# Pauses of the merged streams per head and per pair, and small products of a hybrid decoder step in column groups

## The chip, the cores and the metric

One core of a Trainium2 chip runs the whole step. The metric is the device time of one execution in microseconds (us). Its engines are named as in the profile: PE (TensorE, matmuls), PEld (its weight loads), DVE (VectorE), ACT (ScalarE), POOL (GpSimd), SP (the queue that issues most DMAs).

## The reference, cut to what matters

One layer of a decoder, for a prompt (16 meta tokens and 512 tokens) and for 8 samples of 8 new tokens each with 2048 cached tokens in pages. Both share all weights. Tokens in all: 512 + 64 + 16 = 592.

```
xn = rmsnorm(x) ; h = xn @ w_in                        # one projection, D = 1024 -> 5640
q, k, v | gdn_qkv, gdn_z, gdn_b, gdn_a | gate_a, gate_b = split(h)
# branch a: differential attention, 4 heads, two maps of 64
a   = softmax(q1 k1') - lam * softmax(q2 k2') ; o_a = rmsnorm(a @ v)
# branch b: gated DeltaNet, 4 heads of 128
qkv = silu(causal_dwconv(gdn_qkv, width 4))            # its last 3 rows are an output
gq, gk = l2norm(.) ; beta = sigmoid(gdn_b)
g   = -exp(a_log) * softplus(gdn_a + dt_bias)          # log decay per token and head
gcum = cumsum(g)  ; decay = exp(gcum_i - gcum_j)       # within a chunk
solve (I + lower(beta k k' * decay)) [u, w] = [beta v, beta k exp(gcum)]
v_new = u - w @ S ; o = (q exp(gcum)) @ S + (q k' * decay) @ v_new
S = S exp(g_last) + (k exp(g_last - gcum))' @ v_new
o_b = rmsnorm(o) * silu(gdn_z)
# merge and FFN
mix = sigmoid(gate_a) * (o_a @ w_a) + sigmoid(gate_b) * (o_b @ w_b)
x  += rmsnorm(mix @ w_out)
x  += rmsnorm((gelu(causal_dwconv(gate)) * up) @ w_down)
```

Each sample brings its own state S (128x128 per head) and each prompt head starts from zero. Everything is fp32 to the outside.

## The kernel before

Activations lie with channels on partitions and tokens along the free dimension. Big products are made in fp32r (one pass) on numbers split into a high part `hi` and a rest `lo`: `hi*hi + hi*lo + lo*hi`, three matmuls for one (`project`, `dense_steps`). A product whose operands are plain fp32 is shown by the profile as two matmul rows.

The program is written as Python generators that are merged into one order. Each `yield d` in a stream says: `d` us of PE work of other streams shall be placed before this stream goes on. `merge` counts PE work as it is emitted (`self.work`: 0.00042 us per moving column for fp32r and for products of at most 32 stationary columns, 0.00168 for other fp32 ones, 0.11 per transpose) and takes, of the streams whose pause is over, the one with the least work done against its weight. The pauses come from one table, `DELAY`, by number. Within this order the framework places the instructions on each engine, and every engine then runs in order.

Stages in order:

- `embed`: load x, normalise, transpose, first query products.
- `da_queries`, `gdn_scalars` (beta and g for all heads: `w_in`'s eight columns for b and a against all tokens, in two halves of 256 and 336), `gdn_consts`.
- Two merged streams. `main` (weight `MAIN_1`, later `MAIN_2`): keys, values and prompt attention of four heads, then the four GDN heads one after another (`gdn_chain`), each merged with the projection of the next head (`gdn_project`). `rest` (weight `REST_W`): attention of the samples in four pairs over the paged cache (`sample_attention`), the gates, and branch a.
- `mix`, `out_proj`, `ffn_in`, `ffn_out`.

In `gdn_chain` for one head: row sums of the decays by a product of `ones` with `gu` (the upper triangle times g), exponentials on ACT, transposes of k, q, v, norms by `rsqrt` (an add on DVE and a power on POOL), `kn` (normalised k) and its transpose `kk`, the triangular solve, then the states of the samples: `zk` holds k and q of the eight samples in a block layout, and eight products of `zk` with the eight states accumulate in one PSUM tile. After that four chunks of the prompt follow one another. Behind them stand the gate (`gdn_gate`) and the transposes of the output `on` into `ob`.

`conv_tile` runs the width-4 convolution of one 128-channel tile (three per head: k, q, v) and keeps the last rows in `tail`; its inner function `rest` transposes `tail` and writes it out on POOL's DMA queue.

Of the kernel before, what the change touches and what calls it, by code (L numbers as in the profile page):

```python
# [9 lines left out]
F32 = mybir.dt.float32  # L10
# [41 lines left out]
def _lay_out_constants():  # L52
# [14 lines left out]
    put("ones", np.ones((128, 128)))  # L67
# [27 lines left out]
    put("zero", np.zeros((128, 1)))  # L95
    put("causal", np.where(i[None, :] > i[:, None], NEG, 0.0))
# [35 lines left out]
    13.61, 3.59, 0.94, 0.6, 6.0, 1.52, 1.66, 1.43, 1.32, 1.05, 0.93, 0.17, 26.0, 0.69, 0.9, 0.77,  # L132
    0.09, 0.85, 0.38, 2.28, 0.14, 0.6, 0.74, 2.36, 6.91, 0.77, 1.4, 5.18, 1.38, 1.46, 12.26,
# [15 lines left out]
REST_W = 165.0  # L149


class Body:
# [39 lines left out]
    def run(self):  # L192
# [6 lines left out]
        self.ident = self.consts[:, 0:128]  # L199
        self.mhalf = self.t(self.cpool, [128, 32], "mhalf")  # L200
# [313 lines left out]
    def gdn_scalars(self, pool):  # L514
# [74 lines left out]
        )  # L589

    def gdn_decays(self):
# [46 lines left out]
    def conv_tile(self, ps, ch, dp, dt):  # L638
# [12 lines left out]
        tail = self.t(pool, [128, 27], "tail", bufs=2)  # L651
        nc.scalar.copy(tail[:, 0:3], pb[:, CS - 3 - o : CS - o])
        nc.scalar.copy(
            tail[:, 3:27].rearrange("p (b j) -> p b j", b=NB),
            pb[:, CS - o : CM - o].rearrange("p (b t) -> p b t", b=NB)[:, :, TS - 3 :],
        )

        def rest():
            tp = self.ps("t")
            self.transpose(tp[:27, :128], tail)  # L660
            rows = self.t(pool, [27, 128], "tailT", bufs=2)
            nc.vector.tensor_copy(rows, tp[:27, :128])
            sl = slice(128 * ch, 128 * ch + 128)
            nc.gpsimd.dma_start(self.o["new_gdn_conv_prompt"][0, 0, :, sl], rows[0:3])
            nc.gpsimd.dma_start(self.o["new_gdn_conv_sample"][0, :, :, sl].rearrange("b j c -> (b j) c"), rows[3:27])

# [19 lines left out]
        return rest  # L686
# [12 lines left out]
    def gdn_project(self, h, st):  # L699
# [8 lines left out]
        rest = None  # L708
        for part in (1, 0, 2):
# [24 lines left out]
    def gdn_chain(self, h, st):  # L734
# [4 lines left out]
        def cols(ap, h=h):  # L739
# [26 lines left out]
        self.mm(rp, self.c("ones"), gu, start=True, stop=True)  # L766
# [27 lines left out]
        yield DELAY[2]  # L794
# [7 lines left out]
        yield DELAY[3]  # L802
# [5 lines left out]
        for e in range(2):  # L808
            self.rsqrt(rr[:, e], ss[:, e], 0.25, EPS, 128, 5)
# [8 lines left out]
        yield DELAY[4]  # L818
# [1465 lines left out]
```

## Time and profile before

| | |
|---|---|
| time, median of 3 runs | 1135.83 us (1135.69 to 1139.21) |
| profiled execution, its own time | 1136.37 us |
| its span | 1134.6 us |
| PE busy, 8263 matmul rows | 1112.5 us |
| PEld busy | 976.8 us |
| DVE busy | 729.3 us |
| ACT busy | 524.7 us |
| POOL busy | 225.8 us |
| HBM over the span | 137 GB/s |

How to read the profile: the span goes from the first to the last instruction of the program. A group of instructions shows line, engine, operation, `out<-in` by the program's names, shapes (for PE: contraction*stationary columns, then the moving operand), count, busy time, mean time of one, idle time of the engine before it and what ended it. In an answer in order of time the first two numbers are start and length. A PE row is longer than its share of PE, because matmuls overlap; the distance from start to start tells the cost. `L273` is the one line that issues every product, `L421` the one that issues every transpose, so PE's groups are told apart by tiles.

### The profile page before, as it was taken

The page shows a single profiled execution, that of the slowest core. Times are in us where ns is not written, and L with a number is a line of the kernel's source. Part 1 is how long each engine was busy: PE and PEld are TensorE (multiplying, and loading weights), DVE is VectorE, ACT ScalarE, POOL GpSimd, SP SyncE. Part 2 cuts the span into 40 slices and gives each one's busy share as a digit, 9 for nine tenths or more (in the row PEclk, how much of TensorE's full clock was granted, in tenths as well). Part 3 has the DMA queues.
Part 4 walks back from the last instruction along what each step waited for, and adds up shares of the span by engine and source line. Part 5 has one row for each costly group of instructions (what it writes and reads, how often), then busy time and mean ns, then how long its engine had stood idle before and what let it go on. Part 6 is the DMA issues. An engine that isn't in the chain of part 4 may idle for free.

```text
span 1134.6 us, 22730 instructions
## 1 busy us (share of the span) xinstructions
PE 1112.5 (98%) x8263; PEld 976.8 (86%) x8263; DVE 729.3 (64%) x1891; ACT 524.7 (46%) x1264; POOL 225.8 (20%) x344
## 2 busy tenths in 40 slices
PE   8999999999999999999999999999999999999997
PEld 6987887787787787689999987899999999988886
DVE  5456666696486377375335575599999999752315
ACT  5244544464365365352324244464555555842311
POOL 3122221020120020010000003344444454300000
PEclk9999999999999999999999999999999999999999
DMA  6376336837846866733234344333333332333213
GB/s 193 83 235 199 102 92 200 261 103 251 246 147 224 283 178 223 251 87 87 50 90 118 105 146 135 102 102 95 94 95 95 95 100 84 116 108 108 84 48 120
DMA packets 167610, 156.97 MB, mean 138 GB/s; under 512 B 12540, under 2 KB 123715, under 8 KB 167498
## 3 DMA queue, kind: packets, MB, share of 16 engines
q1 hardware_dynamic: 162833, 147.14, 42.5%
q0 software_dynamic: 3264, 5.16, 1.5%
q10 hardware_dynamic: 1400, 3.22, 0.9%
q8 instruction: 65, 1.06, 0.4%
q14 instruction: 48, 0.39, 0.1%
HBM read 145.60 MB, written 9.88 MB: 137 GB/s over the span
## 4 chain that ended last, share of the span: by engine, by line
PE 82%; DVE 7%; issue 3%; ACT 3%; POOL 3%; DMA 2%; SPq 0%; DVEq 0%; POOLq 0%; ACTq 0%
PE ps_d L273 32%; PE ps_t L273 20%; PE ps_g L273 16%; PE ps_s L273 7%; PE ps_t L421 6%; ACT KT L1421 1%; PE ps_m L273 1%; DVE wlo L316 1%; DVE cy L672 1%; POOL grr L385 1%; DMA wraw<-in_w_ffn_in 1%; DMA page<-in_cache_v 0%; DVE gf L1745 0%; DVE fy L1926 0%; DVE row L992 0%
## 5 line engine op out<-in xcount | busy, mean ns | idle before, releaser
L273 PE MATMUL ps_d<-xhi,whi 128*128 128x256 f32 (+2 forms) x704 | 217.3, 309 | 0.6 <-ACT xhi L315 0.5
L273 PE MATMUL ps_d<-xhi,wlo 128*128 128x256 f32 (+2 forms) x704 | 213.0, 303 | 0.5 <-POOL wlo L316 0.5
L273 PE MATMUL ps_d<-xlo,whi 128*128 128x256 f32 (+2 forms) x704 | 212.4, 302 | 0.3 <-DVE xlo L316 0.3
L316 DVE TENSOR_TENSOR wlo<-wraw,whi 128x512 fp32r<-128x512 f32 x190 | 143.5, 772 | 107.2 <-ACT whi L315 106.3
L315 ACT CAST whi<-wraw 128x512 fp32r<-128x512 f32 x194 | 116.5, 621 | 163.7 <-PE ps_d L273 69.4
L273 PEld LDWEIGHTS ps_d<-xhi,whi 128*128 128x128 f32 x704 | 133.1, 189 | 6.2 <-issue 3.8
L273 PEld LDWEIGHTS ps_d<-xlo,whi 128*128 128x128 f32 x704 | 133.4, 190 | 3.2 <-issue 2.4
L273 PEld LDWEIGHTS ps_d<-xhi,wlo 128*128 128x128 f32 x704 | 133.2, 189 | 2.4 <-issue 1.0
L316 DVE TENSOR_TENSOR lw<-sw,hw 128x512 fp32r<-128x512 f32 x76 | 69.8, 918 | 5.2 <-ACT hw L315 5.2
L1421 ACT COPY KT<-ps_t 128x512 f32<-128x512 f32 x106 | 57.2, 603 | 31.6 <-PE ps_t L421 31.1
L421 PE MATMUL ps_t<-consts,page 128*128 128x128 f32 x512 | 67.8, 279 | 0.5
L273 PE MATMUL ps_t<-fhit,hw 128*128 128x290 f32 x228 | 68.1, 299 | 0.1
L273 PE MATMUL ps_t<-flot,hw 128*128 128x290 f32 x228 | 67.7, 297 | 0.0
L273 PE MATMUL ps_t<-fhit,lw 128*128 128x290 f32 x228 | 67.7, 297 | 0.0
L421 PEld LDWEIGHTS ps_t<-consts,page 128*128 128x128 f32 x512 | 55.5, 140 | 14.1 <-issue 7.0
L315 ACT CAST hw<-sw 128x512 fp32r<-128x512 f32 x76 | 46.7, 617 | 18.5 <-PE ps_g L273 12.2
L273 PEld LDWEIGHTS ps_t<-fhit,hw 128*128 128x128 f32 x228 | 43.0, 189 | 0.4 <-DVE p L1949 0.4
L273 PEld LDWEIGHTS ps_t<-flot,hw 128*128 128x128 f32 x228 | 43.3, 190 | 0.0
L273 PEld LDWEIGHTS ps_t<-fhit,lw 128*128 128x128 f32 x228 | 43.1, 189 | 0.0
L1924 ACT ACTIVATE fy<-fpre,fw 128x592 f32<-128x592 f32 x22 | 19.5, 884 | 46.3 <-DVE fpre L1884 46.3
L1926 DVE SCALAR_TENSOR_TENSOR fy<-fpre,fw,fy 128x592 f32<-128x592 f32 x44 | 36.5, 829 | 1.0 <-ACT fy L1924 0.3
L273 PE MATMUL ps_s<-page,pT 128*32 128x256 f32 x512 | 35.1, 385 | 2.0 <-DMA page<-in_cache_v 1.8
(691 smaller groups left out, 2870.0 us busy)
## 6 DMA issues: line engine op xcount, KB each, us to landing
page<-in_cache_k SPq DMA_DIRECT2D x128, 256.0 KB, 4.4
page<-in_cache_v SPq DMA_DIRECT2D x128, 256.0 KB, 4.2
wraw<-in_w_in SPq DMA_DIRECT2D x88, 256.0 KB, 3.1
wraw<-in_w_ffn_in SPq DMA_DIRECT2D x50, 256.0 KB, 3.0
wraw<-in_w_down SPq DMA_DIRECT2D x44, 256.0 KB, 2.8
raw<-in_w_ffn_in SPq DMA_DIRECT2D x38, 256.0 KB, 2.9
wraw<-in_w_out SPq DMA_DIRECT2D x16, 256.0 KB, 3.2
x<-in_x_prompt SPq DMA_DIRECT2D x4, 512.0 KB, 6.8
```

Of the source, the lines that this page charges most:

```text
L273: return self.nc.tensor.matmul(out, lhsT, rhs, **kw).ins
L315: self.nc.scalar.copy(hi, raw)
L316: (eng or self.nc.vector).tensor_tensor(out=lo, in0=raw, in1=hi.bitcast(F32), op=ALU.subtract)
L385: nc.gpsimd.tensor_tensor(out=dst, in0=dst, in1=self.mhalf[:rows, :n], op=ALU.pow)
L421: self.nc.tensor.transpose(out, in_, self.ident[:k, :k])
L672: nc.vector.scalar_tensor_tensor(out=y, in0=pre[:, j : j + n], scalar=self.cw[:, ch, 24 + j : 25 + j], in1=y, op0=ALU.mult, op1=ALU.add)
L1421: copy(kt[:, :, 128 * j : 128 * j + 128], tp)
L1924: nc.scalar.activation(y, pre[:, 0:592], AF.Identity, bias=fw[:, m, 19:20], scale=fw[:, m, 16:17])
L1926: nc.vector.scalar_tensor_tensor(out=y, in0=pre[:, j : j + 592], scalar=fw[:, m, 16 + j : 17 + j], in1=y, op0=ALU.mult, op1=ALU.add)
```

## The change

- `DELAY` becomes four tables, one per head (GDN head `h`, prompt attention head, or pair of samples `pr`), with two new numbers: 31 (between the value steps of sample attention, zero in all four, where `yield 0.0` stood) and 32 (behind the gate of a GDN head; 0, 0, 0.29, 0). `REST_W` goes from 165.0 to 163.1.
- Beta and decay: the eight columns of weights are put into a tile of 32 columns (24 of them zero) for each of the eight blocks of 128 input channels. Each block is multiplied in fp32 with the hi part and the lo part of x; block k goes to column group k % 4, that is to PSUM rows 32(k % 4) and up. The four groups are summed and transposed by one product with a new constant `sums`.
- States: instead of eight products with 128 columns, each column group takes the four states whose columns fall into it: sixteen products of 32 columns.
- Row sums of the decays: `g` is split into hi and lo (fp32r), `gu` is made twice, and two fp32r products with an fp32r tile of ones take the place of one fp32 product. The constant `ones` leaves the constants; the tile is made on POOL.
- Convolution tails: the three tiles of a head share one tile `tail` of 81 columns, with one transpose, one copy and four DMAs per head.
- The two `rsqrt` of k and q in a head become one over ten columns.
- In `prompt_rows` the transpose for the meta tokens takes 128 columns instead of 16, of which 16 are used.

```diff
 DELAY = (
-    13.61, 3.59, 0.94, 0.6, 6.0, 1.52, 1.66, 1.43, 1.32, 1.05, 0.93, 0.17, 26.0, 0.69, 0.9, 0.77,
-    0.09, 0.85, 0.38, 2.28, 0.14, 0.6, 0.74, 2.36, 6.91, 0.77, 1.4, 5.18, 1.38, 1.46, 12.26,
+    (
+        16.02, 5.28, 1.42, 0.6, 6, 1.52, 1.66, 1.43, 0.33, 0.47, 0.93, 0.17, 26, 0.79, 0.72, 1.17, 0.09, 0.42, 0.38,
+        2.28, 0.07, 0.6, 0.74, 1.49, 8.09, 0.77, 1.4, 5.18, 1.38, 1.46, 12.26, 0, 0,
+    ),
+    (
+        16.02, 2.2, 1.42, 0.87, 6, 1.52, 1.66, 1.43, 0.38, 0.47, 0.93, 0.17, 26, 0.79, 2.06, 1.17, 0.09, 0.42, 0.38,
+        2.28, 0.09, 0.6, 0.74, 1.49, 6.91, 0.77, 1.4, 5.18, 1.38, 1.46, 12.26, 0, 0,
+    ),
+    (
+        16.02, 5.28, 1.42, 0.6, 6, 1.52, 1.66, 1.08, 0.38, 0.47, 0.77, 0.17, 26, 0.79, 0.72, 1.17, 0.09, 0.42, 0.38,
+        2.28, 0.09, 0.6, 0.74, 1.49, 6.91, 0.77, 1.4, 5.18, 1.38, 0.76, 12.26, 0, 0.29,
+    ),
+    (
+        21.53, 5.28, 1.42, 1.56, 6, 1.52, 1.66, 1.43, 0.38, 0.47, 0.93, 0.34, 26, 0.79, 0.72, 1.17, 0.09, 0.42, 0.38,
+        2.28, 0.09, 0.6, 0.74, 1.49, 6.91, 0.77, 1.4, 5.18, 1.38, 1.46, 12.26, 0, 0,
+    ),
 )
-REST_W = 165.0
+REST_W = 163.1
...
-        hi = self.t(pool, [128, 8, 8], "bahi", F32R)
-        lo = self.t(pool, [128, 8, 8], "balo", F32R)
-        nc.vector.tensor_copy(hi, raw)
-        nc.vector.tensor_tensor(out=lo, in0=raw, in1=hi.bitcast(F32), op=ALU.subtract)
-        bat = self.t(pool, [8, NT], "bat")
+        wide = self.t(pool, [128, 8, 32], "baz")
+        nc.gpsimd.memset(wide, 0.0)
+        nc.gpsimd.tensor_copy(wide[:, :, 0:8], raw)
+        bat = self.t(pool, [128, NT], "bat")
         for c in HALF_T:
-            p = self.ps("d")[:8, : c[1] - c[0]]
-            self.project(p, ([hi[:, k] for k in range(8)], [lo[:, k] for k in range(8)]), self.x, c)
+            p = self.ps("d")[:, : c[1] - c[0]]
+            for j, x in enumerate(self.part(self.x, c)):
+                for k in range(8):
+                    r = slice(32 * (k % 4), 32 * (k % 4) + 32)
+                    self.mm(p[r], wide[:, k], x.bitcast(F32)[:, k], start=j == 0 and k < 4, stop=j == 1 and k >= 4)
...
-            self.transpose(p[:n, i, :], bat[:, c0 : c0 + n])
+            self.mm(p[:n, i, :], bat[:, c0 : c0 + n], self.c("sums"), start=True, stop=True)
...
-        gu = self.t(pool, C4, "dd")
-        nc.vector.tensor_tensor(
-            out=gu, in0=self.c("upper").unsqueeze(1).to_broadcast(C4), in1=cols(self.g), op=ALU.mult
-        )
+        gus = []
+        for g, tag, bufs in ((self.ghi, "dd", 1), (self.glo, "lm", 2)):
+            gu = self.t(pool, C4, tag, F32R, bufs=bufs)
+            nc.vector.tensor_tensor(
+                out=gu, in0=self.c("upper").unsqueeze(1).to_broadcast(C4), in1=cols(g.bitcast(F32)), op=ALU.mult
+            )
+            gus.append(gu)
...
-        self.mm(rp, self.c("ones"), gu, start=True, stop=True)
+        for j, gu in enumerate(gus):
+            self.mm(rp, self.ones, gu, start=j == 0, stop=j == 1)
...
-        for e in range(2):
-            self.rsqrt(rr[:, e], ss[:, e], 0.25, EPS, 128, 5)
+        self.rsqrt(rr.rearrange("p e c -> p (e c)"), ss.rearrange("p e c -> p (e c)"), 0.25, EPS, 128, 10)
...
-        for b in range(NB):
-            self.mm(
-                p[:, :128], self.zk[:, 128 * b : 128 * b + 128], state[:, b], start=b == 0, stop=b == NB - 1
-            )
+        for j in range(4):
+            for e in range(4):
+                b = j + 4 * (e % 2)
+                self.mm(
+                    p[32 * e : 32 * e + 32, :128], self.zk[:, 128 * b + 32 * e : 128 * b + 32 * e + 32], state[:, b],
+                    start=j == 0, stop=j == 3,
+                )
...
         yield from self.gdn_gate(h, z2)
+        yield DELAY[h][32]
...
-            self.transpose(tq[:NM, :128], at[:, 0:NM])
+            self.transpose(tq[:, :128], at[:, 0:128])
```

The tails: `conv_tile` no longer returns `rest`, and `gdn_project` ends with one call for the head:

```diff
-        yield DELAY[0]
-        rest()
+        yield DELAY[h][0]
+        self.conv_tails(h, tail)
...
+    def conv_tails(self, h, tail):
+        nc, pool = self.nc, self.gproj
+        tp = self.ps("t")
+        self.transpose(tp[:81, :128], tail)
+        rows = self.t(pool, [81, 128], "tailT")
+        nc.vector.tensor_copy(rows, tp[:81, :128])
+        sl = slice(128 * h, 128 * h + 128)
+        to = self.o["new_gdn_conv_prompt"][0, 0].rearrange("j (p c) -> p j c", p=3)[:, :, sl]
+        nc.gpsimd.dma_start(to, rows[0:9])
+        for p in range(3):
+            to = self.o["new_gdn_conv_sample"][0, :, :, 512 * p + 128 * h : 512 * p + 128 * h + 128]
+            nc.gpsimd.dma_start(to.rearrange("b j c -> (b j) c"), rows[9 + 24 * p : 33 + 24 * p])
```

More of the change, by code (lines that the diff above doesn't have):

```diff
@@ L589, in gdn_scalars @@
         )
+        one = self.t(pool, [128, 128], "one")
+        nc.gpsimd.memset(one, 1.0)
+        nc.gpsimd.tensor_copy(self.ones, one)
+        self.ghi, self.glo = (self.t(self.keep, [128, 4, H], f"g{p}", F32R) for p in ("hi", "lo"))
+        nc.vector.tensor_copy(self.ghi, self.g[:, 0:4])
+        nc.vector.tensor_tensor(out=self.glo, in0=self.g[:, 0:4], in1=self.ghi.bitcast(F32), op=ALU.subtract)
     def gdn_decays(self):
@@ L599, in gdn_decays @@
         p = self.ps("t")[:, : 8 * nch].rearrange("p (c e) -> p c e", e=8)
-        for e, (whole, tail) in enumerate((("upper", "upper_t"), ("ones", "same_t"))):
+        for e, (whole, tail) in enumerate(((self.c("upper"), "upper_t"), (self.ones.bitcast(F32), "same_t"))):
             sl = slice(4 * e, 4 * e + 4)
-            self.mm(p[:, 0:4, sl], self.c(whole), self.g[:, 0:4, :], start=True, stop=True)
+            self.mm(p[:, 0:4, sl], whole, self.g[:, 0:4, :], start=True, stop=True)
             self.mm(p[:NTL, 4, sl], self.c(tail, NTL), self.g[:NTL, 4, :], start=True, stop=True)
@@ L650, in conv_tile @@
         nc.vector.tensor_copy(pre[:, 17:19], pb[:, CM - o : CM + 2 - o])
-        tail = self.t(pool, [128, 27], "tail", bufs=2)
-        nc.scalar.copy(tail[:, 0:3], pb[:, CS - 3 - o : CS - o])
+        part = ch // 4
+        nc.scalar.copy(tail[:, 3 * part : 3 * part + 3], pb[:, CS - 3 - o : CS - o])
         nc.scalar.copy(
-            tail[:, 3:27].rearrange("p (b j) -> p b j", b=NB),
+            tail[:, 9 + 24 * part : 33 + 24 * part].rearrange("p (b j) -> p b j", b=NB),
             pb[:, CS - o : CM - o].rearrange("p (b t) -> p b t", b=NB)[:, :, TS - 3 :],
         )
[L658 to L665, printed above, removed]
         n = 531 + 88 - 3
@@ L707, in gdn_project @@
         outs = {0: (full(q), q[:, CS:NT]), 1: (full(kt), kt[:, CS:NT]), 2: (full(vt), vt[:, CS:NT])}
-        rest = None
+        tail = self.t(pool, [128, 81], "tail")
         for part in (1, 0, 2):
@@ L712, in gdn_project @@
             yield from self.dense_steps(wt, self.x, HALF_T[0], out)
-            if rest:
-                rest()
             yield 0.0
             yield from self.dense_steps(wt, self.x, HALF_T[1], out)
-            rest = self.conv_tile(out, 4 * part + h, *outs[part])
+            self.conv_tile(out, 4 * part + h, *outs[part], tail)
             yield 0.0
-        yield DELAY[0]
-        rest()
+        yield DELAY[h][0]
+        self.conv_tails(h, tail)
     def gdn_gate(self, h, z2):
@@ L817, in gdn_chain @@
         )
-        yield DELAY[4]
+        yield DELAY[h][4]
         p = self.ps("t")
@@ L861, in gdn_chain @@
         nc.scalar.copy(qS, p[64:128, :128])
-        yield DELAY[6]
+        yield DELAY[h][6]
         p = self.ps("g")
@@ L866, in gdn_chain @@
         nc.scalar.copy(v[:NTL], p[:NTL, :128])
-        yield DELAY[7]
+        yield DELAY[h][7]
         p = self.ps("g")
@@ L889, in gdn_chain @@
             vms.append((b4, vm))
-        yield DELAY[8]
+        yield DELAY[h][8]
         def states():
@@ L906, in gdn_chain @@
             )
-            yield DELAY[9]
+            yield DELAY[h][9]
             if i == 1:
@@ L914, in gdn_chain @@
             nc.scalar.copy(v, p[:, :128])
-            yield DELAY[10]
+            yield DELAY[h][10]
             p = self.ps("g")
@@ L927, in gdn_chain @@
             S = S2
-            yield DELAY[11]
+            yield DELAY[h][11]
         nc.gpsimd.dma_start(o["new_gdn_prompt"][0, 0, h], S)
@@ L1008, in gdn_base @@
         res.update(lt=lt, at=at, ltt=ltt, att=att, y=xy, xyt=xyt)
-        yield DELAY[12]
+        yield DELAY[res["h"]][12]
     def gdn_solve(self, res):
@@ L1046, in gdn_solve @@
         nc.scalar.copy(c, cp[:, :, :w])
-        yield DELAY[13]
+        yield DELAY[res["h"]][13]
         for j, s in enumerate(LEVELS[128]):
@@ L1055, in gdn_solve @@
                 lm = level(j + 1)
-            yield DELAY[14]
+            yield DELAY[res["h"]][14]
             dp = self.ps4("g")[:, :, :w]
@@ L1066, in gdn_solve @@
             c, w = c2, 2 * w
-            yield DELAY[15]
+            yield DELAY[res["h"]][15]
             tp = self.ps4("t")
@@ L1084, in gdn_solve @@
         nc.scalar.copy(x[0:64, :, 0:64], tp[:64, :, :64])
-        yield DELAY[16]
+        yield DELAY[res["h"]][16]
         dp = self.ps4("g")
@@ L1192, in da_keys @@
                     nc.scalar.copy(full[:, c[0] : c[1]], p)
-                yield DELAY[21] if half is HALF_T[1] else 0.0
+                yield DELAY[0][21] if half is HALF_T[1] else 0.0
             if part == 0:
@@ L1284, in meta_attention @@
         self.head_norm(pool, os[0:8])
-        yield DELAY[22]
+        yield DELAY[0][22]
         tp = self.ps("t")
@@ L1295, in prompt_attention @@
         self.head_norm(pool, on)
-        yield DELAY[23]
+        yield DELAY[h][23]
         tp = self.ps4("t")
@@ L1445, in sample_attention @@
             rs = self.soft(S, m1, 0)
-            yield DELAY[27]
+            yield DELAY[pr][27]
             acc = self.ps("s")
@@ L1463, in sample_attention @@
                 nc.scalar.copy(pT, tp)
-                yield DELAY[28]
+                yield DELAY[pr][28]
                 for j0 in (0, 2):
@@ L1485, in sample_attention @@
                 self.head_norm(pool, os)
-                yield DELAY[30]
+                yield DELAY[pr][30]
                 tp = self.ps("t")
```

38 lines of the change are left out of this document (19 added, 19 removed).

## The prediction

> **What bounds the kernel now.** I read the page first (busy shares, slices, granted clock), then the sums by stretch, then the waits of PE, and last the order of time at the places that the change touches.
>
> ```profile
> span 1134.6 us, 22730 instructions
> ...
> PE 1112.5 (98%) x8263; PEld 976.8 (86%) x8263; DVE 729.3 (64%) x1891; ACT 524.7 (46%) x1264; POOL 225.8 (20%) x344
> ...
> PEclk9999999999999999999999999999999999999999
> ```
> TensorE is busy for 98% of the span, and its clock was granted in full in every slice. A busy PE is not yet a full one, so the stretches come next. Their columns are the length, the busy time of each engine with its instructions, the granted clock, the DMA share and GB/s.
>
> ```profile
> 0.00:52.00 52.00, 47.77 (x312) 39.90 (x313) 25.56 (x79) 21.73 (x45) 10.24 (x21) 1.00 0.52 150
> 52.00:206.00 154.00, 150.37 (x1240) 124.07 (x1239) 96.20 (x359) 72.34 (x193) 36.94 (x77) 1.00 0.53 162
> 206.00:500.00 294.00, 287.18 (x2580) 227.24 (x2579) 189.69 (x649) 152.15 (x433) 37.18 (x65) 1.00 0.66 210
> 500.00:630.00 130.00, 129.16 (x981) 126.34 (x980) 62.83 (x168) 47.08 (x111) 5.48 (x5) 1.00 0.33 87
> 630.00:1134.60 504.60, 498.05 (x3160) 459.25 (x3158) 355.03 (x639) 231.34 (x485) 136.02 (x179) 1.00 0.33 101
> ```
> The first stretch is the embedding, the queries and the beta/decay product; 52 to 630 holds the two merged streams (keys, prompt attention and the four GDN heads on one side, sample attention, gates and branch A on the other); after 630 come the mix, the output projection and the FFN. From 52 to 630 PE stood idle for 3.63 + 6.82 + 0.84 = 11.3 us. That is all that a new timing of the streams can win there. What PE waited for:
>
> ```profile
> PE ps_t L421 <- DVE on L935: 2.0, 2, 1.3
> PE ps_t L421 <- DVE on L1366: 1.8, 3, 0.9
> PE ps_s L273 <- DMA page<-in_cache_v: 1.8, 2, 1.4
> PE ps_t L421 <- DVE kn L814: 1.2, 1, 1.2
> ```
> These are total, count and longest. They are short and few. PE works in order and hardly ever waits, so PE work that is taken out moves everything behind it forward, and the sum is made of PE work first and of pauses second.
>
> **Beta and decay (gdn_scalars).** Before: 48 products with 8 stationary columns, 24 for each half of the tokens. After: 32 products with 32 columns, in fp32, spread over four column groups. The first stretch below shows the products of before (first, last, and the transposes behind them); the other two rows show the nearest thing to the new ones.
>
> ```profile
> 42.62 0.28 PE L273 MATMUL ps_d<-xhi,bahi 128*8 128x256 f32 x1
> ...
> 48.88 0.32 PE L273 MATMUL ps_d<-xhi,balo 128*8 128x336 f32 x1
> 49.13 0.29 PE L421 MATMUL ps_t<-consts,bat 8*128 8x8 f32 x2
> 49.28 0.41 PE L421 MATMUL ps_t<-consts,gcw 28*128 28x28 f32 x4
> ...
> 255.18 1.94 PE L273 MATMUL ps_s<-KT,qb 128*32 128x256 f32 x32
> 257.05 0.33 PE L421 MATMUL ps_t<-consts,page 128*128 128x128 f32 x1
> ```
> The products of before hold PE from 42.62 to 49.13, 6.51 us. An fp32 product stands as two rows: the value products of sample attention are 4 x 4 x 4 x 4 = 256 by the code and 512 by the page.
>
> ```profile
> L273 PE MATMUL ps_s<-page,pT 128*32 128x256 f32 x512 | 35.1, 385 | 2.0 <-DMA page<-in_cache_v 1.8
> ```
> So the 32 rows of KT,qb are 16 products of 32 columns and 256 tokens, in four column groups: exactly one first half of the new form, and they take 257.05 - 255.18 = 1.87 us. The second half has 336 tokens: 1.87 x 336/256 = 2.45. Together 4.32, a gain of 2.19. Against it, five transposes of 8 rows (0.15 for two, 49.13 to 49.28, thus some 0.1 each with the change of form) become five fp32 products with 128 stationary columns, ten rows; such rows stand 0.106 apart in the state product below, so 1.06 instead of 0.5. Net gain 1.65 us, of 2.2 at the most; the other end is a rival below. DVE loses the two operations that split the weights, POOL gets a memset and a copy; POOL has nothing else to do there (10.24 of 52 us busy).
>
> **States (gdn_chain).** Eight fp32 products of 128 columns per head become sixteen of 32 columns, four column groups in four rounds.
>
> ```profile
> 554.60 1.95 PE L273 MATMUL ps_g<-st,zk 128*128 128x128 f32 x16
> 556.30 0.37 PE L273 MATMUL ps_d<-xhi,whi 128*128 128x256 f32 x1
> ...
> 357.51 0.43 PE L273 MATMUL ps_s<-kTs,qb 128*32 128x64 f32 x16
> 357.87 0.30 PE L273 MATMUL ps_g<-dd,lm 128*128 128x32 f32 x1
> ```
> Before: 1.70 us for 16 rows, 0.106 each. No row has 32 columns by 128 in four groups; the bounds are 64 moving columns (0.36 for 16 rows, so 0.72 for 32) and 256 (1.87 for 32). I take a line between them, 0.72 + 1.15/3 = 1.10, since the cost must grow with the columns, and add 0.1 for going into another form (an estimate, as for the transposes above). Gain 0.5 us a head, 2.0 for four; the bounds give between 3.5 gained and 1.1 lost.
>
> [...] The trace has 32 rows in 1.87 us where rows of the full width would need 32 x 0.225 = 7.2 (0.45 us for 512 columns, below), so the four groups run at 96% of four times the speed. [...] The rows are of this very form, so I keep 96%.
>
> **Row sums of the decays (gdn_chain).** One fp32 product of 512 columns per head becomes two in fp32r, on a hi and a lo part.
>
> ```profile
> 312.12 1.06 PE L273 MATMUL ps_g<-dd,consts 128*128 128x512 f32 x2
> 313.02 0.27 PE L421 MATMUL ps_t<-consts,kt 128*128 128x128 f32 x1
> ...
> 668.13 11.12 PE ps_t L273 x48
> ```
> Two rows take 0.90 us before; 48 fp32r products of 512 columns in a row take 11.12 (a row of the chain), 0.232 each, so 0.46 after. Gain 0.44 a head, 1.75 in all. DVE makes one more 128x512 tile per head, at about the 772 ns of the page's weight splits:
>
> ```profile
> L316 DVE TENSOR_TENSOR wlo<-wraw,whi 128x512 fp32r<-128x512 f32 x190 | 143.5, 772 | 107.2 <-ACT whi L315 106.3
> ```
> DVE is busy 190 of 294 us there, and the pause behind it (DELAY 1) is 3.59 before and 5.28 after for three heads; covered there. In head 1 the pause falls to 2.2, and 0.8 us could show. If no cover held, 3.1 us.
>
> **Convolution tails.** Twelve transposes, copies and pairs of DMAs become four transposes and four copies with four DMAs each.
>
> ```profile
> 316.29 0.28 PE L273 MATMUL ps_d<-xhi,wlo 128*128 128x256 f32 x1
> 316.40 0.27 PE L421 MATMUL ps_t<-consts,tail 128*27 128x128 f32 x1
> 316.43 0.40 PE L273 MATMUL ps_d<-xhi,whi 128*128 128x336 f32 x1
> 316.67 0.31 PE L273 MATMUL ps_d<-xlo,whi 128*128 128x336 f32 x1
> ```
> Without the transpose, the two products beside it would need 0.11 (316.29 to 316.40) and 0.16; 316.67 - 316.29 = 0.38, so one transpose costs 0.11 us and eight fewer give 0.9. POOL's queue loses eight DMA issues of some 0.5 us; nobody waits for them. The prompt's tile of 16 columns transposed as 128 (prompt_rows) keeps its moving columns: nothing either way. The constants are 120 columns fewer in a load that no one waits for: nothing.
>
> **One power instead of two (grr).** Two rsqrt over 5 columns become one over 10.
>
> ```profile
> L385 POOL TENSOR_TENSOR grr<-grr,mhalf x8: 1162/1203/1797, 239.4 to 501.7; 128x5 f32<-128x5 f32 x8
> L554 POOL TENSOR_TENSOR sqb<-beta,half x1: 3543/3543/3543, 52.3 to 52.3; 128x20 f32<-128x20 f32 x1
> 326.24 2.95 POOL L385 TENSOR_TENSOR grr<-grr,mhalf 128x5 f32<-128x5 f32 x2 [4.51 <-DVE grr L384]
> 329.22 0.17 DVE L813 TENSOR_SCALAR cq<-grr 128x5 f32<-128x5 f32 x1 [0.98 <-POOL grr L385]
> 329.54 0.27 DVE L814 TENSOR_SCALAR kn<-kn,kc 80x128 f32<-80x128 f32 x1
> 329.95 0.26 PE L421 MATMUL ps_t<-consts,kn 80*128 80x80 f32 x1 [1.24 <-DVE kn L814]
> ```
> Between 1.2 us (5 columns) and 3.5 (20), a line gives 2.0 for 10. In head 1, above, kn stands on DVE behind cq, which waits for the second power; one power of 2.0 for 2.95 brings kn 0.9 us earlier, and PE waits 0.9 less. A head where kn is ahead of cq needs the first power alone: there kn comes 0.8 later. I take 0.5 us gained, between 0.9 and a loss of 0.8.
>
> **The pauses.** A pause ends when that much PE work of other streams is placed, and a stream places a whole step: 12 products of 256 columns count 12 x 256 x 0.00042 = 1.29, 24 count 2.58, 16 page transposes 1.76. A pause above zero and below 1.29 therefore mostly buys the same one step, and most new values (8, 9, 13, 14, 17, 20) stay below it or cross it barely. Three I can place. The new pause behind the gate (32) is 0.29 in head 2, where the longest wait for L935 is (1.3 us): one step covers it, 1.3 gained; the other heads stay without. Pause 23 (head norm, L1366) falls from 2.36 to 1.49: both fit into one step of 2.58, but a page step (1.76) covers only the new one, so a wait may grow by 0.9, at four heads 3.5 at the worst. Pauses 0, 1 and 2 move tails and chain starts by a step, with other work there to fill. Sum taken: 1.3 gained, between the 11.3 us of idle time and 5 lost.
>
> **The sum.** 1.65 + 2.0 + 1.75 + 0.9 of PE work is 6.3 us; with 0.5 and 1.3 of waits 8.1. The profiled execution took 1136.37 us with a span of 1134.6, against a median of 1135.83, so its terms can be taken off the median: 1127.7, at a span near 1126.5.
>
> **Rivals.** (1) *PE is not what binds 206 to 500.* Weight loads fill only 227 of 294 us there, so there could be room, and what is taken from PE between 52 and 630 would come back as waiting for the chain of small steps. Left would be the 1.65 us of the beta product: 1134.2, no measurable change. Against it: 6.8 us idle in 294. [...] Chance 0.05. (2) *New waits eat the gain.* The order of the streams changes at many places; the four waits in the list are 6.8 us in all, and as much again in new places leaves 1134.5. The pages speak most for it: 0.66 DMA share, and PE waited 1.8 us for cache_v. Against it: 8 us less in 448 asks only 2% more of the DMAs. Chance 0.12. (3) *Slower: the column groups do not run together*, for the beta and the state products, because of their operands. Rows would cost 0.225 (256 columns) and 0.106 (128): 32 x 0.225 + 32 x 0.295 = 16.6 us in place of 4.3, and 3.4 in place of 1.2 a head: 21 us more than my sum, 1149. It decides when fewer than two of four overlap. Against it stand the 32 rows in 1.87 us. Chance 0.02. (4) *Slower by the pauses alone*: pause 23 and its like open 11 us of waits more than they close, against 1.8 us at this place now; 1140. Chance 0.06. (5) *The new timing also takes out half of the idle 11.3 us*: some 5 us below my sum, 1122. Chance 0.17.
>
> **How the numbers follow.** My forecast has the rest, 0.58, with its own range of 1123.5 to 1132 from the bounds of states, power and pauses. 0.3% of this time is 3.4 us, about what a measurement of this kernel tells from no change. Faster (below 1132.4): forecast nearly whole plus (5), 0.75. Within: (1), (2) and a rest of the forecast, 0.17. Slower: (3), (4), 0.08. The range for 8 in 10 reaches from 1120 (into case 5) to 1134.5 (case 2).
>
> **What would show it.** Beta: 32 products as 64 rows of 128*32 in about 4.3 us before the tail products, and 52 us reached 1.6 us earlier. States: 32 rows per head in about 1.1 us. Row sums: two rows of 512 columns 0.23 apart. One grr power of 2 us per head. Idle PE time from 52 to 630 near 9.5 us. I am wrong if that idle time rises by more than 5 us, or if a new name leads the waits of PE; wrong on the groups if rows of 128*32 stand 0.1 us apart one by one.

## The result and the profile after

| | before | after |
|---|---|---|
| time, median, first chip | 1135.69 us | 1130.35 us, ratio 0.9949, 95% interval 0.9938 to 0.996 |
| time, median, second chip (run `after_again`) | 1136.82 us | 1128.87 us, ratio 0.993, interval 0.9915 to 0.9945 |
| profiled execution: time, span | 1136.37, 1134.6 us | 1129.95, 1128.2 us |
| TensorE (PE) busy | 1112.5 us | 1104.1 us |
| TensorE idle between 52 and 630 us | 11.3 us | 12.4 us |

The change makes the kernel 5 to 8 us faster; 1127.7 was forecast. Of the seven executions behind the 1130.35, one took 4431 us; the ratio is formed without it. The page after, its first lines and the clock:

```profile
span 1128.2 us, 22859 instructions
...
PE 1104.1 (98%) x8340; PEld 972.2 (86%) x8340; DVE 728.9 (65%) x1883; ACT 525.0 (47%) x1264; POOL 224.2 (20%) x336
...
PEclk9999999999999999999999999999999999999999
```

Busy time fell by 8.4 us although there are 77 rows more, and the granted clock (the share of TensorE's full clock that the profile records) is full in every slice, as before (its mean is 0.998 in both). The sums by stretch of the changed kernel, with the columns as in the prediction:

```profile
52.00:206.00 154.00, 150.56 (x1234) 124.51 (x1233) 98.26 (x378) 72.18 (x197) 34.19 (x73) 1.00 0.53 164
206.00:500.00 294.00, 286.17 (x2672) 230.58 (x2671) 191.43 (x635) 154.44 (x435) 38.82 (x56) 1.00 0.67 211
500.00:630.00 130.00, 128.89 (x996) 125.76 (x995) 63.26 (x166) 45.47 (x106) 2.71 (x3) 1.00 0.33 88
```

Idle TensorE time is 3.44 + 7.83 + 1.11 = 12.4 us: the new timing took no waiting away. What TensorE waits for in the changed kernel (total, times, longest):

```profile
PE ps_t L436 <- DVE on L1396: 2.3, 3, 0.9
...
PE ps_d L288 <- DVE wlo L331: 1.5, 1, 1.5
PE ps_s L288 <- DMA page<-in_cache_v: 1.2, 2, 0.7
PE ps_t L436 <- DVE on L964: 1.1, 2, 0.6
...
PE ps_t L436 <- DVE kn L841: 0.9, 1, 0.9
PE ps_t L436 <- DVE kn L840: 0.7, 1, 0.7
```

L1396, L964, L840 and L841 are L1366, L935, L814 and L815 of before. The second row shown is new: at 409.1 us TensorE waits 1.5 us for a weight split of the last head's projection, which stands in DVE's queue behind the start of the third head's chain. It becomes the key to the experiments. The changed products in order of time (start, length, what):

```profile
42.42 1.07 PE L288 MATMUL ps_d<-xhi,baz 128*32 128x256 f32 x16
43.31 1.05 PE L288 MATMUL ps_d<-xlo,baz 128*32 128x256 f32 x16
44.69 1.34 PE L288 MATMUL ps_d<-xhi,baz 128*32 128x336 f32 x16 [0.33 <-DVE qm L1180]
45.82 1.34 PE L288 MATMUL ps_d<-xlo,baz 128*32 128x336 f32 x16
47.09 0.61 PE L288 MATMUL ps_t<-consts,bat 128*128 128x8 f32 x4
47.63 0.92 PE L436 MATMUL ps_t<-consts,gcw 28*128 28x28 f32 x12
...
305.52 0.39 PE L288 MATMUL ps_g<-dd,ones 128*128 128x512 f32 x1
305.75 0.39 PE L288 MATMUL ps_g<-lm,ones 128*128 128x512 f32 x1
305.98 0.32 PE L288 MATMUL ps_d<-xhi,wlo 128*128 128x336 f32 x1
...
552.96 1.08 PE L288 MATMUL ps_g<-st,zk 128*32 128x128 f32 x32
553.97 0.39 PE L288 MATMUL ps_d<-xhi,whi 128*128 128x256 f32 x1
```

Beta and decay hold TensorE from 42.42 to 47.09, less a wait of 0.33: 4.34 us. The convolution weights' transposes behind them (gcw) begin at 47.63, before at 49.28. The row sums take 305.98 - 305.52 = 0.46, the states 553.97 - 552.96 = 1.01 us.

### The profile page after: what moved, and what is told of

It reads as the page before. It is cut to its first block, busy times and chain, and to the rows that moved or that the text cites. A ratio compares the mean times of both kernels' runs of the same rounds, so it can differ in the third digit from the quotient of the medians.

```text
span 1128.2 us, 22859 instructions
## 1 busy us (share of the span) xinstructions
PE 1104.1 (98%) x8340; PEld 972.2 (86%) x8340; DVE 728.9 (65%) x1883; ACT 525.0 (47%) x1264; POOL 224.2 (20%) x336
## 4 chain that ended last, share of the span: by engine, by line
PE 80%; DVE 9%; issue 3%; ACT 3%; DMA 2%; POOL 2%; DVEq 0%; SPq 0%; ACTq 0%; POOLq 0%
PE ps_d L288 31%; PE ps_t L288 20%; PE ps_g L288 15%; PE ps_s L288 7%; PE ps_t L436 6%; PE ps_m L288 1%; DVE wlo L331 1%; DVE cy L685 1%; DMA wraw<-in_w_out 1%; ACT KT L1451 1%; POOL grr L400 1%; DVE lw L331 0%; DVE gf L1775 0%; DMA page<-in_cache_v 0%; DMA wraw<-in_w_ffn_in 0%
## 5 line engine op out<-in xcount | busy, mean ns | idle before, releaser
L288 PE MATMUL ps_t<-fhit,lw 128*128 128x290 f32 x228 | 67.7, 297 | 0.0
L959 POOL DMA_DIRECT2D out_new_gdn_sample<-st x4 | 3.8, 952 | 162.4 <-DVE st L925 134.0
```

Of the source, the lines that this page charges most:

```text
L288: return self.nc.tensor.matmul(out, lhsT, rhs, **kw).ins
L959: nc.gpsimd.dma_start(o["new_gdn_sample"][0, :, h].rearrange("b k v -> k b v"), state)
```

## The experiments

Three questions were open: which half of the change carries the gain, what the new wait for the weight split costs, and why the lead over before, 7.9 us up to 765 us, was only 6.4 us from 779 us on.

| kernel | time, us | ratio to before (95%) | idle TensorE, 52 to 630 | clock at 0.50 before the end |
|---|---|---|---|---|
| `pauses_only` | 1140.83 | 1.0038 (1.0024 to 1.0052) | 15.6 | 3.41 us |
| `products_only` | 1143.05 | 1.0062 (1.0042 to 1.0082) | 17.5 | 3.41 us |
| `rest_w` | 1153.22 | 1.0155 (1.0136 to 1.0175) | 19.6 | 20.5 us |
| `no_pause32` | 1135.18 | 0.9984 (0.9974 to 0.9994) | 14.2 | 3.41 us |
| `two_powers` | 1136.09 | 0.9996 (0.9986 to 1.0006) | 14.5 | 6.83 us |
| `two_powers_pool` | 1140.13 | 1.0012 (0.9999 to 1.0026) | 13.8 | 13.65 us |
| `after_pool` | 1140.11 | 1.0023 (1.0012 to 1.0034) | 15.9 | 10.24 us |
| `gap_probe` | 1136.74 | 0.9993 (0.9984 to 1.0002) | 12.4 | 10.24 us |
| `old_beta` | 1131.28 | 0.9946 (0.9934 to 0.9959) | 12.9 | none |
| `fetch_moved` | 1130.31 | 0.9947 (0.9931 to 0.9962) | 12.4 | none |
| `fetch_16` | 1129.53 | 0.9936 (0.9922 to 0.995) | 13.3 | none |
| `after_again` | 1128.87 | 0.993 (0.9915 to 0.9945) | 12.6 | none |

The last two columns are of the profiled executions (one for each kernel; the times are medians of 5 to 12); the clock column adds up the trace's records of a granted clock below 1, without the one behind the last products (0.50 from 1131.0 us in before, from 1123.7 in the changed kernel). The medians of before on these three chips are 1136.69, 1137.19 and 1136.82 us, so kernels of different groups are better compared by their ratios. Three groups shared a chip each: `pauses_only`, `products_only`, `two_powers`, `fetch_moved`; `two_powers_pool`, `after_pool`, `gap_probe`, `old_beta`; `after_again`, `fetch_16`, `rest_w`, `no_pause32`.

### The two halves

`pauses_only`, before with the new table:

```diff
-DELAY = (13.61, 3.59, 0.94, ...)
+DELAY = ((16.02, 5.28, 1.42, ..., 0, 0), ...)   # four rows, as in the change
-REST_W = 165.0
+REST_W = 163.1
```

> The kernel before with the new pauses alone (four rows of DELAY, the yields 31 and 32, REST_W 163.1); no product changes. Theory (the removed TensorE work carries the gain, the pauses carry next to nothing): 1135 to 1136.5 us, within 0.3% of 1135.7, idle TensorE time between 52 and 630 us within 1.5 us of the 11.3 us of before. Rival A (the pauses carry a part of the gain, as the 1.3 us of the prediction): 1134.0 to 1134.6 us, idle time about 10 us. Rival B (the new pauses do harm that the smaller products outweigh; the changed kernel's idle time there rose from 11.3 to 12.4 us): 1136.5 to 1138 us, the wait for the evacuation after pause 23 (L1366 of the old text) well above its 1.8 us.

`products_only`, the changed kernel with the old table:

```diff
-DELAY = ((16.02, 5.28, 1.42, ..., 0, 0), ...)
+OLD = (13.61, 3.59, 0.94, ..., 0, 0)
+DELAY = (OLD,) * 4
-REST_W = 163.1
+REST_W = 165.0
```

> The changed kernel with the old pauses in all four rows (new yields 0, REST_W 165.0). Theory: 1129.5 to 1131 us, the changed kernel's 1130.35 within 0.1%, so that the products alone explain the 5.3 us. Rival A (1.3 us come from the pauses): 1131.3 to 1132 us. Rival B (the new pauses do harm): 1127.5 to 1129 us, and less idle TensorE time between 52 and 630 us than the changed kernel's 12.4 us.

The theory fell, and so did rival A; rival B has the direction right for the first kernel and wrong for the second. Each half alone makes the kernel slower, by 4 and by 6 us, and both together make it 5 to 8 us faster. The sums by stretch of `products_only`, and its waits for the split and for kn:

```profile
52.00:206.00 154.00, 149.97 (x1235) 124.68 (x1238) 95.54 (x357) 72.49 (x194) 35.16 (x70) 1.00 0.52 161
206.00:500.00 294.00, 280.61 (x2594) 221.30 (x2587) 184.21 (x631) 146.08 (x405) 35.20 (x58) 0.99 0.66 209
500.00:630.00 130.00, 129.90 (x1004) 126.61 (x1004) 67.00 (x180) 50.35 (x134) 4.68 (x4) 1.00 0.31 80
```

```profile
PE ps_d L275 <- DVE wlo L318: 2.1, 2, 1.9
...
PE ps_t L423 <- DVE kn L827: 1.7, 2, 1.4
```

TensorE idles 13.4 us between 206 and 500, before 6.8, and the clock there is not full (0.99). The order itself costs too. `products_only` makes the very products of the changed kernel, and its page has

```profile
PE 1111.5 (97%) x8340; PEld 975.8 (85%) x8340; DVE 730.5 (64%) x1883; ACT 524.8 (46%) x1264; POOL 222.1 (19%) x336
```

TensorE is busy 7.4 us longer than the 1104.1 of the changed kernel, for the same rows. The stretch of half clock, 3.41 us at 0.50, is 1.7 of that; the other 5.7 us come from the order alone. With the 5.1 us more of idle time (17.5 for 12.4) this is 12.5 of the 13.5 us between the two spans. `pauses_only` shows the other side: its busy time is 1111.5 too, 1.0 below before in spite of 1.7 us for half clock, but its idle time is 4.3 us above.

The largest part of the order's effect can be seen in one place: the score and value products of the samples are the same 1024 rows everywhere. Their groups (count, then busy us and mean ns between the bars, then idle time before them), first of before, then of after, then of `products_only`:

```profile
L273 PE MATMUL ps_s<-KT,qb 128*32 128x256 f32 x512 | 35.7, 385 | 0.6
```

```profile
L288 PE MATMUL ps_s<-KT,qb 128*32 128x256 f32 x512 | 34.1, 385 | 0.5 <-DVE smx L1282 0.2
L288 PE MATMUL ps_s<-page,pT 128*32 128x256 f32 x512 | 33.6, 384 | 1.2 <-DMA page<-in_cache_v 1.2
```

```profile
L275 PE MATMUL ps_s<-KT,qb 128*32 128x256 f32 x512 | 36.7, 385 | 0.7
L275 PE MATMUL ps_s<-page,pT 128*32 128x256 f32 x512 | 35.6, 384 | 1.9 <-DMA page<-in_cache_v 1.9
```

70.8 us before (with the 35.1 that the prediction shows), 67.7 after, 72.3 in `products_only`. These busy times count the overlap of each run's last rows with what follows; from start to start the rows take 66.2, 62.9 and 66.3 us. In the order of time, 16 such rows in a row take 1.00 us and 32 take 1.86, but a run cut to 10, 12 or 14 rows still takes 0.98 to 1.03 (one of 8 takes 0.57). So on these rows the order is worth 3.5 us between the last two kernels before any wait is counted. `merge` places by counted PE work, and the products changed that count: with the old pauses the streams meet at other places.

`rest_w`, the smallest piece of the new timing undone alone:

```diff
-REST_W = 163.1
+REST_W = 165.0
```

> The changed kernel with REST_W back from 163.1 to 165.0, the smallest piece of the new timing by itself; no product changes, but 870 of some 7300 TensorE rows are placed elsewhere, from the first heads on. Theory (the new numbers fit this program and no other, so one of them undone costs several us): 1134 to 1143 us. Rival (pauses and weights are a second-order matter, as the prediction's 1.3 us for all of them has it): within 1.5 us of the changed kernel.

The direction is the theory's, the size is beyond it: 24 us slower than `after_again` on the same chip. From 206 to 500 us:

```profile
206.00:500.00 294.00, 279.45 (x2552) 218.64 (x2552) 181.66 (x614) 143.65 (x400) 35.66 (x55) 0.97 0.65 207
```

TensorE idles 14.6 us there and the clock falls to a mean of 0.97; over the span it is at 0.50 for 20.5 us, which alone takes some 10 us. The two longest waits, 2.93 us at 443.6 us and 3.19 us at 631.0 us, go with it: the clock falls within the first and 1.6 us behind the second.

`no_pause32`, the new pause behind the third head's gate:

```diff
-        2.28, 0.09, 0.6, 0.74, 1.49, 6.91, 0.77, 1.4, 5.18, 1.38, 0.76, 12.26, 0, 0.29,
+        2.28, 0.09, 0.6, 0.74, 1.49, 6.91, 0.77, 1.4, 5.18, 1.38, 0.76, 12.26, 0, 0,
```

> The changed kernel without the new pause behind the gate of the third head (0.29 to 0); TensorE's rows differ at 23 places, all behind that head. Prediction's step: the wait for the output's normalisation there comes back, 1.3 us slower, 1131.6 us. Theory of an order that fits this program alone: anything from 0.5 faster to 5 slower, with the difference in waits between 480 and 630 us. Rival (the pause does nothing by now): within 0.3 us.

```profile
PE ps_t L436 <- DVE on L964: 2.7, 2, 2.0
```

The wait named in the prediction came back, 2.7 us in place of 1.1. It lasts 2.04 us at 485 us, and behind it the clock is at 0.50 for 3.41 us. At 480 us TensorE loses 4.4 us against `after_again`; the medians differ by 6.3, a little past the theory's 5. A further 1.6 us of the difference in the traces (7.5 in all) arise behind 760 us, where the weight transfer that a later section treats takes 5.0 us.

### The wait for the split and the clock

`two_powers`, two rsqrt over 5 columns again. It changes no PE work, yet the framework then orders TensorE's rows differently at some 100 places, from 248 us on.

```diff
-        self.rsqrt(rr.rearrange("p e c -> p (e c)"), ss.rearrange("p e c -> p (e c)"), 0.25, EPS, 128, 10)
+        for e in range(2):
+            self.rsqrt(rr[:, e], ss[:, e], 0.25, EPS, 128, 5)
```

> The changed kernel with the two powers over 5 columns each in place of the one over 10. In the changed kernel the one power took 1.98 to 3.21 us and the normalisation kn cost TensorE 0.94 us in head 0 and 1.02 us in head 1, in the kernel before 1.24 and 0.34 us. As the prediction has it (one power gains 0.5 us): 1130.8 to 1131 us. Rival (the one power is slower for the key half, which kn needs first): 1129.6 to 1130.2 us, and the waits on kn get shorter. Null: 1130.35 within 0.2 us, because what is gained in head 0 is lost in head 1.

All three expectations missed: 5.7 us slower than the changed kernel's 1130.35 (and 5.8 slower than `fetch_moved` below, the changed kernel with a few small products more, on the same chip). The stretch around the split, in steps of 2 us (the granted clock is the third number from the end):

```profile
410.00:412.00 2.00, 0.00 (x0) 0.00 (x0) 2.00 (x8) 1.80 (x6) 0.00 (x0) 1.00 0.00 0
412.00:414.00 2.00, 1.16 (x4) 0.87 (x5) 2.00 (x6) 1.34 (x9) 1.68 (x2) 0.64 0.02 4
414.00:416.00 2.00, 2.00 (x11) 1.78 (x11) 1.05 (x3) 0.87 (x6) 0.93 (x1) 0.50 0.96 197
416.00:418.00 2.00, 2.00 (x11) 2.00 (x11) 0.17 (x1) 1.31 (x7) 1.15 (x1) 0.50 0.88 328
418.00:420.00 2.00, 2.00 (x12) 2.00 (x12) 1.91 (x6) 0.37 (x1) 0.46 (x2) 0.65 1.05 339
420.00:422.00 2.00, 2.00 (x15) 2.00 (x15) 0.53 (x4) 0.00 (x0) 1.10 (x1) 1.00 0.53 118
```

DVE is busy without a break while TensorE stands still: here the wait for the split is 3.02 us, in the changed kernel 1.50. Then the clock stands at half: (0.36 + 0.50 + 0.50 + 0.35) x 2 = 3.4 us of TensorE time lost. 1.5 + 3.4 = 4.9 of the 5.7 us in this execution.

`gap_probe` forces such a pause where nothing else changes:

```diff
             self.drain(product(0))
+            late = self.t(pool, [128, 512], "late", bufs=1)
+            p = self.ps("s")
+            nc.tensor.matmul(p[:8, :8], ones[:, :8], ones[:, :8], start=True, stop=True)
+            nc.vector.tensor_copy(late[:8, :8], p[:8, :8])
+            for _ in range(6):
+                nc.vector.tensor_copy(late, lnb[:, 0:512])
+            nc.tensor.matmul(p[:8, :8], late[:1, :8], ones[:, :8], start=True, stop=True)
```

> The changed kernel with one forced pause of TensorE in the embedding, near 19 us: a product of 8 x 8, a DVE copy of it, six DVE copies of 128x512, and a product of 8 x 8 that reads the last copy; their results are unused, and the order of all other rows of TensorE is that of the changed kernel. The pause should be some 4.5 us. Theory (a pause of TensorE much above 1.7 us makes the granted clock fall to 0.50 for one or two stretches of 3.41 us): the clock falls there, and the time grows by the pause and by 1.7 or 3.4 us more: 1136.5 to 1138.5 us. Rival (the low clock near 415 us came from something else): clock 1.00 throughout, 1134.5 to 1135.2 us.

```profile
15.00:18.00 3.00, 1.01 (x10) 0.78 (x8) 2.62 (x5) 1.26 (x3) 0.00 (x0) 1.00 0.34 86
18.00:21.00 3.00, 0.39 (x3) 0.36 (x4) 2.51 (x5) 0.00 (x0) 0.30 (x1) 0.54 0.00 0
21.00:24.00 3.00, 3.00 (x15) 3.00 (x15) 2.55 (x3) 1.84 (x3) 2.73 (x3) 0.50 0.10 12
24.00:27.00 3.00, 3.00 (x23) 3.00 (x23) 1.92 (x4) 1.45 (x4) 1.29 (x4) 0.82 0.83 220
...
189.00:192.00 3.00, 1.23 (x18) 0.50 (x16) 3.00 (x8) 0.14 (x1) 0.00 (x0) 1.00 0.98 291
192.00:195.00 3.00, 3.00 (x18) 2.44 (x14) 0.39 (x1) 0.72 (x1) 0.00 (x0) 0.55 1.03 339
```

The theory held: the pause was 4.60 us, the clock fell to 0.50 at 18.23 us for 6.83 us, and from 50 us on TensorE stood 6.6 us behind the changed kernel. A second fall was not planned: a page wait of 1.77 us at 189 us was followed by 3.41 us of half clock, and from 200 us on TensorE stood 8.4 us behind, so a part of the 1136.74 belongs to it.

The low stretches are 3.41, 6.83, 10.24 or 13.65 us long in all runs, one to four times 3.413, and the two falls in this run are 192.31 - 18.23 = 174.08 us apart, 51 times 3.413. In every run with several falls, the one at the end among them, they begin whole multiples of 3.413 us apart, to within 0.01 us. So in these traces the clock changes on a grid of 3.413 us; by what rule it falls, they do not show. Waits of 1.77 us (`gap_probe`), 1.90 (`products_only`), 2.04 (`no_pause32`), 2.14 (`pauses_only`), 3.02 (`two_powers`) and 3.19 (`rest_w`) were followed by a clock of 0.50. The length alone does not settle it. A wait of 1.96 us at 185 us (`old_beta`) lay across a point of the grid and was followed by a full clock, but so was one of 1.90 us (`after_pool`) that lay between two.

The split moved off DVE's queue, in the changed kernel (`after_pool`) and in `two_powers` (`two_powers_pool`):

```diff
-            wt = self.weight(w, C_G + 512 * part + 128 * h)
+            raws = self.raw_w(w, C_G + 512 * part + 128 * h)
+            wt = self.split_w(raws, eng=self.nc.gpsimd if (h, part) == (3, 0) else None)
```

> The changed kernel with the same weight split on POOL. There the wait is 1.50 us and the clock stays full. Theory: 1.5 us less, 1128.9 us. Rival (POOL needs 1.29 us for a tile against 0.68 on DVE, and the order of TensorE changes at 42 places behind it, so another wait takes its place): 1130 to 1131 us.

> The kernel with two powers, with one weight of the last head's projection (the second of three) split into hi and lo on POOL instead of DVE, so that TensorE need not wait for DVE's queue there (3.02 us at 410 us with two powers, after which the granted clock stood at 0.50 for 6.83 us). Theory (the wait and the slow clock behind it make the loss): both go, 3.0 + 3.4 us less than 1136.1, so 1129.7, and with TensorE's rows reordered at 32 places up to 1132. Rival 1 (the wait costs its length and the clock has another cause): 1133.1 us, the clock falls to 0.50 all the same. Rival 2 (the loss sits in the other places where the order differs from the changed kernel's): 1135.5 to 1136.5 us.

Every expectation for the two missed. The wait at 410 us was gone in both, but the last head's chain was then placed otherwise, and near 468 us the clock fell, for 6.83 and 13.65 us, though no single wait there was above 0.93 us: TensorE stood still for 1.41 and 1.33 us of the 3.41 before, in pieces. `after_pool` became 10 to 11 us slower than the changed kernel. `two_powers_pool` is not clearly slower than `two_powers`: 1140.13 stands against 1136.09 on another chip, but the intervals of the two ratios overlap. Its executions fall into two groups, and the profiled one is the slowest: with a mean clock of 0.998 or 0.999 five took 1135.4 to 1138.3 us, with 0.992 to 0.996 seven took 1140.1 to 1143.2. So the half clock comes and goes from execution to execution of one kernel and makes some 4.5 us here. Without it this kernel is still no faster than `two_powers`, so its new order seems to cost what the missing wait saves; that is not shown further. `after_pool` had one more low stretch, 3.41 us at 51 us, behind small products and hardly any standing still. What exactly brings the half clock stays open: from one point of the grid to the next, 1.3 to 2.7 us of standing still were followed by it, but up to 1.9 us in other places were not, nor 2.2 to 2.6 in the first 4 us of the program.

### One part undone with the order held

`old_beta` has the beta/decay product of before; it lies ahead of the merged streams, and behind it TensorE's rows keep their order.

```diff
-            for j, x in enumerate(self.part(self.x, c)):
-                for k in range(8):
-                    r = slice(32 * (k % 4), 32 * (k % 4) + 32)
-                    self.mm(p[r], wide[:, k], x.bitcast(F32)[:, k], start=j == 0 and k < 4, stop=j == 1 and k >= 4)
+            self.project(p, ([hi[:, k] for k in range(8)], [lo[:, k] for k in range(8)]), self.x, c)
```

> The changed kernel with the beta/decay product of before (48 products with 8 stationary columns, five transposes). TensorE's order is otherwise the changed kernel's, so this is one part undone with the order held. By the prediction's terms (4.32 for 6.51 us, 0.5 us more for the transposes): 1.65 us slower, 1132.0 us. Rival 1 (what TensorE gains there is lost in waiting later): 1130.2 to 1130.7 us. Rival 2 (as in the two halves of the change, an order that does not fit costs more than the part): over 1134 us.

The median rose by 0.93 us against the changed kernel's first chip, and its ratio to before, 0.9946, is close to the first chip's 0.9949 but 1.8 us above the second's 0.993; so the times neither show the 1.65 us nor exclude them. In the trace TensorE stands 1.5 us further behind after the product (from 0.84 to 2.35), as forecast, and 1.3 us of the loss are won back at 750 to 800 us, at the place of the next two runs. States and row sums cannot be undone this way, since the order moves with them; what they gain is read from the traces alone.

### What was given back in the feed-forward part

`fetch_moved` (32 products) and `fetch_16` (16) put small products at the very start:

```diff
+            p = self.ps("s")
+            for _ in range(32):
+                nc.tensor.matmul(p[:8, :8], ones[:, :8], ones[:, :8], start=True, stop=True)
             for c in (0, 512, D):
```

> The changed kernel with 32 products of 8 x 8 by 8 columns added at the very start (the embedding), their result unused; every other instruction and order is as in the changed kernel. The 128 TensorE instructions move each later instruction fetch of 16 KB by about half of its spacing (17 us in the feed-forward part), so that none falls into the 256 KB transfer of the first feed-forward weight at 746 us. Theory (that fetch slowed the transfer from 3.0 to 4.7 us, and the 1.5 us that the changed kernel gives back between 765 and 779 us come from it): issue to landing of that weight is 3.0 to 3.4 us, the lead over before stays near 7.9 us past 779 us, 1128.6 to 1129.4 us (1.5 us gained, at most 0.5 us paid for the added products). Rival (the transfer is slow because it starts on an idle queue, or from memory, at random): the landing stays at 4.5 us or scatters, time 1130.3 to 1130.9 us.

> The changed kernel with 16 products of 8 x 8 by 8 columns at its very start (64 TensorE instructions in place of the 128 of the earlier try, in the 2.3 us in which TensorE waits for the first row). The fetch before the first feed-forward weight moves some 4 us forward, to 745 us, out of the transfer. Theory: landing 2.8 to 3.1 us, and 0.8 to 1.4 us less than the changed kernel on the same chip. Rival: the fetch still touches the transfer, or the products cost what it gains: within 0.4 us.

> The changed kernel unaltered, as the base for the other three on the same chip, and for a second profile of it. Theory (an instruction fetch of TensorE falls into the transfer of the first feed-forward weight, at a place that the program fixes): the fetch near 749 us and a landing of 4.2 to 4.8 us again, 1130 to 1131 us. Rival (that slow transfer was an accident of one execution): landing near 3.0 us.

The DMA view of 746 to 752 us, first the changed kernel, then `fetch_moved` (queue and kind; the weight's row ends with the us from issue to landing):

```profile
q8 instruction: 1, 0.02, 1.0%
...
wraw<-in_w_ffn_in SPq DMA_DIRECT2D x3, 256.0 KB, 4.7
```

```profile
wraw<-in_w_ffn_in SPq DMA_DIRECT2D x2, 256.0 KB, 2.8
```

The instruction fetch (16 KB for some 254 TensorE instructions) at 749.1 us is gone from the transfer, which lands in 2.8 us; `fetch_16` gives 3.05. Over all the profiles that show it, the landing is 2.8 to 3.05 us without a fetch in the transfer and 3.4 to 5.0 with one. So the mechanism held in the traces: where the changed kernel's lead over before falls by 1.5 us, it falls by 0.3 in `fetch_moved` and `fetch_16`. The price did not show in the times. `after_again`, with nothing changed, has the fetch 0.3 us later in the transfer, lands in 3.39 and loses only 0.2 there, so the loss is not fixed by the program; `fetch_moved` stood 1.4 us behind the changed kernel from 21 us on; and `fetch_16` at 1129.53 is no faster than `after_again` at 1128.87. No version beat the changed kernel.

## Why the prediction was right or wrong

- **Time.** 1127.7 for 1130.35 and 1128.87: the sum of 8.1 us stands against 5.3 and 8.0 measured. That it came so near is in part luck. The terms of the products came to 6.5 us for 6.3 by errors that cancel, the 1.8 us for the power and the pauses did not come as reckoned, and the order brought some 2 us of TensorE's time that the sum did not have (the 8.4 us of busy time less 6.5).
- **Beta and decay**: right. 4.34 us for 4.32; the groups run together. The ten small rows behind them took 1.00 us from start to start for 0.49 before, so 1.66 us were gained for 1.65. That what follows began just 1.65 us earlier (49.28 to 47.63) is chance: the products began 0.20 us earlier, waited 0.33, and only four of the ten rows stand ahead of it.
- **States**: right in mechanism, too small. 1.01 for 1.10 in the last head; over the four heads the distances from start to start fell from 7.68 to 4.26 us, 3.4 us for the forecast 2.0.
- **Row sums**: 0.46 as forecast in the head shown, 0.55 in the other three, for some 0.90 before; 1.5 in all for 1.75.
- **Tails and meta tokens**: the tails' distances fell from 0.76 to 0.30, half of the 0.9. The transposes of 128 in place of 16 columns, costed at nothing, went from 1.81 to 2.29, 0.5 us lost.
- **One power**: wrong term. 128x10 took 2.0 to 3.2 us:

```profile
L400 POOL TENSOR_TENSOR grr<-grr,mhalf x4: 1981/2552/3213, 238.1 to 495.5; 128x10 f32<-128x10 f32 x4
```

  The line between two rows gave the lowest value; kn cost TensorE 0.9 + 0.7 us in two heads, where one head had cost 1.2. No 0.5 us was gained.
- **The pauses**: this step failed. It read them as worth 1.3 us, because most stay below one step of work. The sentence that the 11.3 us of idle time are all that a new timing can win does not hold: the order changes how long TensorE takes for the same rows (5.7 us between `products_only` and the changed kernel) and whether its clock stays full. Pause 32 had the right mechanism, but the 2.0 us wait it covers costs 4.4 us in the trace with the half clock behind it, not 1.3; REST_W, which the prediction did not cost at all, costs 24 us when it alone is set back. The pauses are not a gain beside the products but the condition for it: alone they cost 4 us, and without them the products cost 6.
- **Idle time**: 12.4 us for 9.5 forecast. The wait for L935 fell (2.0 to 1.1), the one for L1366 grew (1.8 to 2.3, at most 0.9 each, as bounded), and the split's 1.5 us is new. What made up for it was a term that the sum lacked: the samples' products lost 3.1 us of busy time (3.4 from start to start) by standing in fuller runs; the other rows gave a part of it back.
- **After 630 us** nothing was to change; in the profiled execution 1.5 us were given back, with a fetch inside the transfer of a weight (4.7 us to landing). In `after_again` (3.39 us) they were not.
- **Rivals.** (1) is refuted: what the products gave up between 52 and 630 us did not come back as waiting, which rose by 1.1 us. (3) is refuted by 4.34 us. (2) fits in part, one new wait of 1.5 us. (4), 1140 us by the pauses alone, is the time of `pauses_only`, 1140.83, but not by its mechanism: the wait at pause 23 rose from 1.8 to 2.4 us only, and the rest came from other waits and 3.41 us of half clock. (5) did not happen, since idle time rose.

## What to carry to other kernels

Where an order is made from counted work, a saved product and the pauses around it are one change: test them together, and expect the order to move as many us as the products do. Here the new table does harm in the kernel before and the old one in the changed kernel; whether another table would have served the new products as well, no run shows. In this kernel waits of TensorE of 1.77 to 3.19 us in six runs were followed by 3.41 us or more at half clock (two of 1.90 and 1.96 us were not), so such a wait was not to be costed at its length alone; look at the granted clock behind it, in steps of 2 us. A term costed at nothing because a pause "buys the same one step" needs the new order in hand, not the rule by which it is made.

## What the hardware showed beyond that

- Half clock came in stretches of 3.41, 6.83, 10.24 or 13.65 us, and the falls of one run began whole multiples of 3.413 us apart (174.08 us, 51 of them, in `gap_probe`). As a rule TensorE had stood still in the 3.41 us before, for as little as 1.33 us in pieces (`two_powers_pool`); once, in `after_pool` at 51 us, it hardly had. At 0.50, 3.413 us cost up to 1.7 us of TensorE time.
- A run of 10, 12 or 14 rows of 128*32 in four column groups took as long as one of 16, 0.98 to 1.03 us (before, at 365.09, 367.14 and 306.89 us among others).
- With one instruction fetch of 16 KB inside it, a 256 KB transfer landed in 3.4 to 5.0 us, without one in 2.8 to 3.05, in the profiles of these kernels.
